# Gate half of a gated MLP's input projection with tokens on partitions: 16 of 48 weight pairs by seven products, results mixed and multiplied there, transposed afterwards

## The chip, the cores and the metric

One core of one Trainium2 chip runs the whole kernel. The metric is device time in microseconds (us) of one execution; lower is better. The time before is the median of three executions, 2474.93 us. Where the text speaks of "no change" it means within 0.2% of that, about 5 us.

## The reference, cut to what matters

Two layers of a trunk over 256 tokens of width 2048. Layer 0 mixes tokens with a spatial gating unit, layer 1 with latent attention; after each comes a gated MLP with a short convolution. The change is in layer 0's mixer alone:

```python
def gmlp_mixer(x, w_in, ln_g, ln_b, w_s, b_s, w_out):
    z = jax.nn.gelu(x @ w_in)                 # 256 x 2048 by 2048 x 12288
    u, v = jnp.split(z, 2, axis=-1)           # 256 x 6144 each
    v = layer_norm(v, ln_g, ln_b)
    v = v.reshape(B, S // GM_BLOCK, GM_BLOCK, GM_GROUPS, GM_GROUP_DIM)   # 2 windows of 128, 8 groups of 768
    w = w_s * mask[None]
    s = jnp.einsum('gij,bnjgd->bnigd', w, v) + jnp.transpose(b_s)[None, None, :, :, None]
    return (u * s.reshape(B, S, GM_HALF)) @ w_out
```

`u` is the gate half and `v` the value half. All products carry about float32 precision: each operand is split into a high and a low part of the type that the matrix engine takes in one pass (`F32R`), and three of the four part products are added: high by high, low by high, high by low.

## The kernel before

Weights stream from memory in chunks of 1 MB (128 partitions x 2048 numbers). `Feed` loads a chunk into `raw` (three buffers, SP's queue), ScalarE casts it to the high part (`wh`, line 128), and VectorE subtracts for the low part (`wl`, line 131). A chunk is split two chunks ahead of its use, into 14 buffers of 1 MB named `big`.

**The value half** (lines 705 to 743) runs in six groups `v0` to `v5` of 1024 columns, each with eight chunks (pairs of row blocks of 128). Tokens are the stationary operand and 512 weight columns move, so results have tokens on partitions: two token blocks by two column halves, four banks `q3`, `p2`, `e`, `q4`, which the code calls DIRECT. A plain pair (`Banks.eight`) is 8 block products of three matmuls, 24 matmuls. For 20 pairs of groups 1 to 5 a Strassen-like scheme with seven block products (`Banks.seven`, 21 matmuls) is used. It needs sums of weight blocks (line 138: `ts`, then `th`, `tl`), sums of token blocks made once (`xc`), four more banks (`p1`, `q5`, `p7`, `p6`, called OWN), and after a group's last such pair four VectorE operations that fold these banks (`rest`, lines 436 to 444). Group results go through Gelu into `v[g]`.

**The gate half** (lines 809 to 832) runs in twelve groups of 512 columns with four chunks each, the other way round (`prod_a`, line 369): weights are stationary and tokens move, so results have features on partitions. A block of 128 x 128 weights takes two matmuls: the high weights against 512 columns (high and low tokens), the low weights against 256. So a chunk is 32 matmuls, half of 512 and half of 256 columns. `sum_halves` adds the two halves. Every second group, `spatial` mixes 1024 columns of `v` by 16 products of 128 columns (tile `s`); `scaled` applies the layer norm's gain and bias per feature (a column of `cst`) and the spatial bias, and line 830 multiplies by the gate, into `pT`, which has features on partitions, as the output projection (`down`, tag `wo`) wants its stationary operand.

Between the halves stand one transpose of the layer norms' rows (line 746), and two products of 512 columns for row sums of the spatial weights (line 753).

The order on each engine is made by the framework's scheduler from the program order and dependencies; an engine then executes its list in order. PSUM has eight banks, given out in rotation by `bank`; a matmul into a bank waits until the readers of its former contents are done. Small tiles rotate too: `t1` (6 buffers), `t2` (5 buffers of 128 x 512).

Of the kernel before, what the change touches and what calls it, by code (L numbers as in the profile page):

```python
# [8 lines left out]
F32 = mybir.dt.float32  # L9
# [40 lines left out]
V_SEVEN = [()] + [(2, 3, 4, 6)] * 5  # L50

# [22 lines left out]
class Feed:  # L74
# [59 lines left out]
    def _seven(self, i, raw):  # L134
# [13 lines left out]
        self.sums = last if i >= 48 else None  # L148
# [64 lines left out]
def trunk(ctx: ExitStack, tc: tile.TileContext, x, xT, gm_in, gm_wout, ffn_up, ffn_dn,  # L213
# [37 lines left out]
    chunks += [(gm_in[i], 2048, "") for i in range(48, gm_in.shape[0])]  # L251
# [34 lines left out]
    def turn(t, k1, k2):  # L286

        b0, b1 = slice(0, P), slice(P, S)
        tc.keep_in_program_order(nc.vector.tensor_tensor(t[:, 0], k1[:, b0], k1[:, b1], ALU.subtract))
        nc.vector.tensor_tensor(t[:, 1], k1[:, b1], k2[:, b1], ALU.subtract)  # L290
        nc.vector.tensor_tensor(t[:, 2], t[:, 1], k1[:, b0], ALU.subtract)
        nc.vector.tensor_tensor(t[:, 3], k2[:, b0], t[:, 2], ALU.add)
# [113 lines left out]
    class Banks:  # L406


        def __init__(self, tag, names):
            self.tag, self.begun = tag, set()  # L410
            self.acc = {n: bank(f"{tag}_{n}") for n in names}
# [5 lines left out]
        def eight(self, a, hi, lo):  # L417

            for b in range(2):
                for f in range(2):  # L420
                    for j in range(len(a[b])):
                        self.to(DIRECT[2 * b + f], a[b][j], hi, lo, j * 1024 + f * 512)

        def seven(self, a, sums, wh, wl, th, tl, turned=0):
            s1, s2, s3, s4 = sums
            self.to("q3", s4, wh, wl, 512)
            self.to("p2", a[0][1], wh, wl, 1024)
            self.to("p1", a[0][0], wh, wl, 0)
# [17 lines left out]
    class Acts:  # L446
# [5 lines left out]
        def make(self, u, kind, tag="big"):  # L452
# [4 lines left out]
            x = self.src[u // 4][:, 2 * u % 8 : 2 * u % 8 + n, :]  # L457
# [17 lines left out]
            nc.scalar.copy(hi, x)  # L475
            tc.keep_in_program_order(nc.vector.tensor_tensor(lo, x, hi.bitcast(F32), ALU.subtract))
# [4 lines left out]
    def down(n_k, src, tag, ln, acts, skew=SKEW):  # L481
# [6 lines left out]
        for hf, units in enumerate(seq):  # L488
            n = len(units)
            last = [u for u, kind in units if kind != "wide"][-1]  # L490
            acc = Banks(f"{tag}{hf}", OWN + DIRECT if hf else DIRECT + OWN)
            for i, (u, kind) in enumerate(units):
# [6 lines left out]
                if left == 6:  # L499
                    ln.prep()  # L500
                a, sums = acts.got[u]
# [202 lines left out]

    for gi in range(6):

        acc = Banks(f"v{gi}", DIRECT if gi == 0 else DIRECT + OWN if gi % 2 else OWN + DIRECT)
        rest = (None,) * 4
        for c, p in enumerate(V_PAIRS[gi]):
# [14 lines left out]
            if c == 4 and gi == 5:  # L724
                wT = slot([P, 2, 1024], "wT")
                wTg = wT[:, 0, :].rearrange("p (g i) -> p g i", g=NG)
                nc.sync.dma_start(wTg, w_sT)
                nc.sync.dma_start(wT[:, 1, :], b_s.to_broadcast([P, 1024]))
                nc.gpsimd.memset(wTg[64:P, :, 0:64], 0.0)
# [8 lines left out]
        if gi == 0:  # L738
            nc.sync.dma_start(cst, consts)
            nc.sync.dma_start(rope_sb, ropes)  # L740

            lnrow = tp.tile([P, P], F32, tag="t1", name="lnrow", bufs=T1)
            nc.sync.dma_start(lnrow, ln_rows.rearrange("r (k p) -> (r k) p", p=P))
    stats(5)
    lnt = bank("lnrowT")
    nc.tensor.transpose(lnt[:, 0:P], lnrow, ident)
    nc.scalar.copy(lncol, lnt[:, 0:P])
    rsum = slot([P, 1024], "rsum")
    ones = tp.tile([P, P], F32, tag="t1", name="ones", bufs=T1)
    nc.gpsimd.memset(ones, 1.0)  # L750
# [16 lines left out]
    def norm_v(gi, b):  # L767
# [4 lines left out]
    for b in range(2):  # L772
        norm_v(0, b)
# [35 lines left out]
    for gi in range(12):  # L809
        acc = [bank(f"u{gi}_{f}") for f in range(4)]  # L810
        for c in range(4):
            hi, lo = feed.next()
            prod_a(acc, xhl, range(4 * c, 4 * c + 4), hi, lo)
            if gi > 0:
                next(jobs, None)
# [465 lines left out]
```

## Time and profile before

| what | us |
|---|---|
| median of three executions | 2474.93 (2474.13 to 2475.21) |
| profiled execution, its own time | 2475.22 |
| span of the profile | 2473.0 |
| value half, groups 1 to 5 (first matmul of `v1` to the transpose of line 746) | 50.77 to 254.77 |
| gate half with what stands between (to the first matmul of `wo`) | 254.77 to 544.87, 290.10 |

PE is TensorE, PEld its weight loads, DVE VectorE, ACT ScalarE, POOL GpSimd, SP the engine that issues most transfers. A matmul's listed duration is its latency, and successive ones overlap; its cost in a stream is the distance between starts. The same holds, less strongly, for DVE and ACT. The timeline merges equal neighbours ("x32") and gives the start of the first and the time to the end of the last.

### The profile page before, as it was taken

Reading aid. Unit: us, or ns where it says so; the run is one execution under the profiler, and the core shown is the slowest. Engines: PE = TensorE matmul, PEld = TensorE weight load, DVE = VectorE, ACT = ScalarE, POOL = GpSimd, SP = SyncE. Lnnn points to the kernel's source line nnn. Section 1 sums busy time; section 2 is a strip of 40 time slices with the busy share of each in tenths; the row PEclk is TensorE's granted clock in tenths of the full one; section 3 lists DMA queues with packets and bytes.
Section 4 is the critical chain, followed back from the end, with each engine's and each line's share of the span. In section 5 each row is a group of like instructions: output and inputs, shape, how many; then the busy total and the mean of one; then the engine's idle time right before and its main releaser. Section 6 shows DMA issues by size and latency. Waiting matters only on the chain. (4 is left out here: it accounts for less than half of the span.)

```text
span 2473.0 us, 33399 instructions
## 1 busy us (share of the span) xinstructions
PE 2460.1 (99%) x12947; PEld 2118.2 (86%) x12947; DVE 1992.8 (81%) x2786; ACT 1425.3 (58%) x1995; POOL 88.3 (4%) x171
## 2 busy tenths in 40 slices
PE   9999999999999999999999999999999999999998
PEld 7888888888888888888888888988888888888886
DVE  7999866679898788788777897866688787878798
ACT  6666544456565656566654466565565665655453
POOL 0000000000000000000000000000000000000000
PEclk9999999999999999999999999999999999999999
DMA  7556544556665678777868885544478787877885
GB/s 281 204 204 218 207 171 171 178 187 215 204 204 204 215 297 323 296 279 288 330 217 325 302 296 191 191 156 158 173 271 314 268 312 293 301 265 277 297 324 199
DMA packets 108990, 606.15 MB, mean 245 GB/s; under 512 B 10272, under 2 KB 11040, under 8 KB 61600
## 3 DMA queue, kind: packets, MB, share of 16 engines
q1 hardware_dynamic: 84832, 463.51, 52.8%
q0 software_dynamic: 24000, 140.52, 14.9%
q8 instruction: 101, 1.65, 0.3%
q14 instruction: 57, 0.47, 0.1%
HBM read 538.98 MB, written 65.01 MB: 244 GB/s over the span
## 5 line engine op out<-in xcount | busy, mean ns | idle before, releaser
L131 DVE TENSOR_TENSOR wl<-raw,wh 128x1024 fp32r<-128x1024 f32 (+4 forms) x693 | 971.9, 1420 | 237.6 <-ACT wh L128 140.2
L128 ACT CAST wh<-raw 128x1024 fp32r<-128x1024 f32 (+4 forms) x693 | 820.7, 1211 | 405.6 <-PE u L233 99.7
L233 PE MATMUL up<-xhl,wh 128*128 128x512 f32 x2624 | 611.3, 390 | 0.0
L233 PEld LDWEIGHTS up<-xhl,wh 128*128 128x128 f32 x2624 | 487.4, 188 | 97.7
L233 PEld LDWEIGHTS up<-xhl,wl 128*128 128x128 f32 x2624 | 325.8, 192 | 6.4
L233 PE MATMUL up<-xhl,wl 128*128 128x256 f32 x2624 | 328.1, 283 | 0.0
L233 PE MATMUL u<-xhl,wh 128*128 128x512 f32 x768 | 180.8, 391 | 0.0
L233 PEld LDWEIGHTS u<-xhl,wh 128*128 128x128 f32 x768 | 142.2, 188 | 28.6 <-DVE v L734 0.2
L128 ACT CAST th<-ts 128x1536 fp32r<-128x1536 f32 x106 | 110.1, 1052 | 87.8 <-DVE ts L138 63.7
L131 DVE TENSOR_TENSOR tl<-ts,th 128x1536 fp32r<-128x1536 f32 x106 | 125.4, 1219 | 8.0 <-PE dn_p L233 3.4
L233 PEld LDWEIGHTS u<-xhl,wl 128*128 128x128 f32 x768 | 95.3, 192 | 1.9
L233 PE MATMUL u<-xhl,wl 128*128 128x256 f32 x768 | 95.9, 283 | 0.0
L233 PE MATMUL mo<-wh,oT 128*128 128x512 f32 x256 | 82.4, 401 | 0.0
L138 DVE TENSOR_TENSOR ts<-ts,raw 128x512 f32<-128x512 f32 x106 | 72.8, 687 | 0.9
L233 PE MATMUL v_q<-wh,xhl 128*128 128x512 f32 x224 | 69.9, 393 | 0.4 <-ACT wh L128 0.4
L138 DVE TENSOR_TENSOR ts<-raw 128x1024 f32<-128x1024 f32 x53 | 64.6, 1219 | 1.2 <-PE wo_q L233 1.0
L233 PE MATMUL v_p<-wh,xhl 128*128 128x512 f32 x192 | 59.7, 390 | 0.6 <-ACT wh L128 0.6
L233 PEld LDWEIGHTS mo<-wh,oT 128*128 128x128 f32 x256 | 45.5, 189 | 7.1
L233 PEld LDWEIGHTS v_q<-wh,xhl 128*128 128x128 f32 x224 | 42.3, 189 | 9.7 <-ACT wh L128 1.1
L233 PE MATMUL mo<-wl,oT 128*128 128x512 f32 x128 | 50.0, 391 | 0.0
L682 ACT ACTIVATE lny<-lnt,lncol 128x128 f32<-128x128 f32 x96 | 36.5, 470 | 15.6 <-PE lnt L678 15.5
L155 DVE TENSOR_TENSOR praw<-praw 128x512 f32<-128x512 f32 x64 | 43.9, 686 | 0.6
(1703 smaller groups left out, 4142.8 us busy)
## 6 DMA issues: line engine op xcount, KB each, us to landing
raw<-in_ffn_up_dram SPq DMA_DIRECT2D x172, 1024.0 KB, 7.0
raw<-in_gm_in_dram SPq DMA_DIRECT2D x93, 1024.0 KB, 4.9
raw<-in_ffn_dn_dram SPq DMA_DIRECT2D x68, 1024.0 KB, 6.8
raw<-in_gm_wout_dram SPq DMA_DIRECT2D x48, 1024.0 KB, 5.4
praw<-in_ffn_dn_dram POOLq DMA_DIRECT2D x16, 1024.0 KB, 14.8
keptth<-pth POOLq DMA_DIRECT2D x16, 1024.0 KB, 8.2
kepttl<-ptl POOLq DMA_DIRECT2D x16, 1024.0 KB, 9.2
fth<-keptth POOLq DMA_DIRECT2D x16, 1024.0 KB, 9.6
```

The lines of the kernel that those rows point to most:

```text
L128: cast = self.nc.scalar.copy(hi, raw)
L131: self.nc.vector.tensor_tensor(lo, raw, hi.bitcast(F32), ALU.subtract)
L138: add = lambda o, a, b: self.nc.vector.tensor_tensor(o, a, b, ALU.add)
L155: add = lambda o, a, b: pin(nc.vector.tensor_tensor(o, a, b, ALU.add))
L233: recent[0] = nc.tensor.matmul(o, l, r, start=start, stop=stop, skip_group_check=True)
L682: nc.scalar.activation(y[:, j], t[:, j * P : (j + 1) * P], AF.Identity, bias=lncol[:, o : o + 1], scale=lncol[:, g : g + 1])
```

## The change

The gate half gets the value half's form. Its 48 weight chunks become six groups of eight pairs, with tokens stationary and 512 weight columns moving; 16 pairs use seven products. A chunk's data is the same, but a pair is now gathered from two stored chunks, in pieces of 1024 numbers instead of rows of 2048. Results have tokens on partitions. So the layer norm's gain and bias become rows: `cst`'s columns are transposed once after `v0`, written to memory (`gbd`), and read back as rows spread over 128 partitions, two of 256 KB for each half group (`row_v`, POOL's queue, tiles of `t2`). `norm_v` applies mean, deviation, gain and bias to `v[g]` in place (eight VectorE operations a group in place of one for each token block). `spatial` makes the spatial weights stationary and moves 512 (or twice 256) columns of `v`; ScalarE adds the spatial bias on the way out of PSUM. The product with the gate goes into `v[g]`, and one group later `turned` transposes its 16 blocks of 128 x 128, and ScalarE copies them back to `v[g]`, which takes `pT`'s place. The eight banks `ub` are used by turns: a group's DIRECT banks are the next group's OWN banks, and `spatial` and `turned` use the OWN banks before the first seven-product pair does. The row sums and `scaled` are gone. The transposes of line 746's kind move to the end of `v0`, in four banks given out there.

```diff
+U_PAIRS = [[0, 1, 5, 7, 2, 6, 3, 4]] + [[0, 1, 2, 5, 3, 7, 4, 6]] * 5
+U_SEVEN = [(2, 3)] + [(2, 3, 4)] * 4 + [(2, 3)]
...
-    chunks += [(gm_in[i], 2048, "") for i in range(48, gm_in.shape[0])]
+    for g in range(6):
+        for p in U_PAIRS[g]:
+            i = 48 + 8 * g + p // 2
+            w = gm_in[i : i + 5 : 4, :, p % 2 * 1024 : p % 2 * 1024 + 1024].rearrange("f p c -> p f c")
+            chunks.append((w, 2048, "seven" if p in U_SEVEN[g] else "wide"))
...
     for gi in range(6):
 
-        acc = Banks(f"v{gi}", DIRECT if gi == 0 else DIRECT + OWN if gi % 2 else OWN + DIRECT)
+        acc = Banks(f"v{gi}", DIRECT if gi == 0 else OWN + DIRECT if gi % 2 else DIRECT + OWN)
...
+            if c == 4 and gi == 0:
+                nc.sync.dma_start(cst, consts)
+                nc.sync.dma_start(rope_sb, ropes)
+                nc.sync.dma_start(lnrow, ln_rows.rearrange("r (k p) -> (r k) p", p=P))
+                nc.sync.dma_start(brow[0:NG, :], b_s.rearrange("o (g i) -> (o g) i", g=NG))
...
         if gi == 0:
...
+            lnt, bst, gbt = bank("lnrowT"), bank("brT"), bank("gbT")
+            bank("spare")
+            nc.tensor.transpose(gbt[0:96, 0:P], cst[:, C_GMG : C_GMG + 96], ident)
+            nc.tensor.transpose(lnt[:, 0:P], lnrow, ident)
+            nc.tensor.transpose(bst[:, 0:NG], brow[0:NG, :], ident[0:NG, 0:NG])
+            gbs = tp.tile([P, P], F32, tag="t1", name="gbs", bufs=T1)
+            nc.scalar.copy(gbs[0:96, :], gbt[0:96, 0:P])
+            nc.gpsimd.dma_start(gbd.rearrange("r (f c) -> (r f) c", c=P), gbs[0:96, :])
+            nc.scalar.copy(lncol, lnt[:, 0:P])
+            nc.scalar.copy(bsc, bst[:, 0:NG])
     stats(5)
-    lnt = bank("lnrowT")
-    nc.tensor.transpose(lnt[:, 0:P], lnrow, ident)
-    nc.scalar.copy(lncol, lnt[:, 0:P])
...
-    for f in range(2):
-        rb = bank(f"rows{f}")
-        mm(rb, ones, wT[:, 0, f * 512 : (f + 1) * 512], True, True)
-        nc.scalar.copy(rsum[:, f * 512 : (f + 1) * 512], rb)
...
+    def row_v(g, f):
+
+        got = []
+        for i in range(2):
+            t = tp.tile([P, 512], F32, tag="t2", name=f"vr{g}{f}{i}", bufs=T2)
+            nc.gpsimd.dma_start(t, gbd[12 * i + 2 * g + f : 12 * i + 2 * g + f + 1, :].to_broadcast([P, 512]))
+            got.append(t)
+        return got
+
+    def norm_v(g, f, rows):
+
+        for b in range(2):
+            t = v[g][:, b, f * 512 : (f + 1) * 512]
+            nc.vector.scalar_tensor_tensor(t, t, mv[b][:, 0:1], rows[0], ALU.subtract, ALU.mult)
+            nc.vector.scalar_tensor_tensor(t, t, vrs[b], rows[1], ALU.mult, ALU.add)
...
+    ub = [bank(f"ub{i}") for i in range(8)]
+
+    def spatial(g, tiles):
+
+        for i, t in enumerate(tiles):
+            b, f = i // 2, i % 2
+            n = 2 * g + f
+            cuts = [(0, 512)] if n % 3 != 1 else [(0, 256), (256, 512)]
+            for o, e in cuts:
+                h = (512 * n + o) // 768
+                mm(t[:, o:e], wTg[h], v[g][:, b, f * 512 + o : f * 512 + e], True, True)
+            for o, e in cuts:
+                h = (512 * n + o) // 768
+                nc.scalar.activation(v[g][:, b, f * 512 + o : f * 512 + e], t[:, o:e], AF.Identity,
+                                     bias=bsc[:, h : h + 1])
+
+    def turned(g, tiles):
+
+        for i, t in enumerate(tiles):
+            src = v[g][:, i // 2, i % 2 * 512 : i % 2 * 512 + 512]
+            for j in range(4):
+                nc.tensor.transpose(t[:, j * P : (j + 1) * P], src[:, j * P : (j + 1) * P], ident)
+            nc.scalar.copy(src, t)
...
+    for g in range(6):
+        direct, own = (ub[4:], ub[:4]) if g % 2 else (ub[:4], ub[4:])
+        acc = Banks(f"u{g}", DIRECT + OWN, direct + own)
+        for c, p in enumerate(U_PAIRS[g]):
+            a = [[x_parts(xhl, 2 * p + j, b) for j in range(2)] for b in range(2)]
+            got = feed.next()
+            if p in U_SEVEN[g]:
+                acc.seven(a, xc[p], *got, turned=512, across=True)
+                if p == U_SEVEN[g][-1]:
+                    rest = acc.rest()
+            else:
+                acc.eight(a, *got, across=True)
+            if c == (0 if g else 2):
+                spatial(g, own)
+            if c == 1 and g:
+                turned(g - 1, own)
+            if c == 1 and g < 5:
+                rows = row_v(g + 1, 0)
+            if c in (3, 5) and g < 5:
+                norm_v(g + 1, c // 4, rows)
+                if c == 3:
+                    rows = row_v(g + 1, 1)
+            if c in (4, 5, 6) and g == 5:
+                acts.make(*plan(NF_GM)[0][c - 4])
+        for n, t in zip(DIRECT, rest):
+            nc.vector.tensor_tensor(t, acc.acc[n], t, ALU.add)
+            nc.scalar.activation(t, t, AF.Gelu_apprx_tanh)
+        for i, t in enumerate(rest):
+            o = v[g][:, i // 2, i % 2 * 512 : i % 2 * 512 + 512]
+            nc.vector.tensor_tensor(o, o, t, ALU.mult)
 
     ln = Norm(0, {})
-    acc, end = down(NF_GM, pT, "wo", ln, acts)
+    acc, end = down(NF_GM, pT, "wo", ln, acts, tiles=ub, beside=lambda: turned(5, ub[4:]))
```

The order of instructions moves at three places that matter. In the rows below a name's last number is the program's own count; `[waits X]` names the engines or queues on whose semaphores the row waits.

On PE, at the end of `v0`: before, the first matmuls of `v1` follow at once.

```order
L233 MATMUL v0_q4_203<-wl7_348,xhl0_3_87 128x512
L233 MATMUL v1_q3_463<-wh8_377,xhl0_0_84 128x512 [waits Activation_49]
L233 MATMUL v1_q3_463<-wh8_377,xhl0_0_84 128x512
L233 MATMUL v1_q3_463<-wl8_378,xhl0_0_84 128x512 [waits DVE_49]
L233 MATMUL v1_q3_463<-wh8_377,xhl0_0_84 128x512 x2
L233 MATMUL v1_q3_463<-wl8_378,xhl0_0_84 128x512
L233 MATMUL v1_p2_464<-wh8_377,xhl0_0_84 128x512 x2
```

After the change three transposes stand between, and `v1`'s first three banks are theirs: `q3` and `p2` wait for ScalarE at their first matmul.

```order
L236 MATMUL v0_q4_207<-wl7_356,xhl0_3_87 128x512
L762 MATMUL gbT_469<-ident_186,cst_183 96x128 [waits DMAHW0_49,Pool_49]
L763 MATMUL lnrowT_467<-ident_186,lnrow_200 128x128 [waits DMAHW2_49]
L764 MATMUL brT_468<-ident_186,brow_201 128x8 [waits DMAHW3_49]
L236 MATMUL v1_q3_483<-wh8_385,xhl0_0_84 128x512 [waits Activation_49]
L236 MATMUL v1_q3_483<-wh8_385,xhl0_0_84 128x512
L236 MATMUL v1_q3_483<-wl8_386,xhl0_0_84 128x512 [waits DVE_49]
L236 MATMUL v1_q3_483<-wh8_385,xhl0_0_84 128x512 x2
L236 MATMUL v1_q3_483<-wl8_386,xhl0_0_84 128x512
L236 MATMUL v1_p2_484<-wh8_385,xhl0_0_84 128x512 [waits Activation_49]
```

On ACT, at the same place, after the change: the copies that empty those banks stand behind the last Gelu of `v0` and a cast; before, the cast `wh10` followed the cast `th9` directly.

```order
L756 ACTIVATE v0_462,vsum_197<-v0_e_206 128x512 [waits PE_49]
L756 ACTIVATE v0_462,vsum_197<-v0_q4_207 128x512 [waits PE_49]
L131 CAST th9_425<-ts9_422 128x512 [waits DVE_49]
L766 COPY gbs_474<-gbT_469 96x128 [waits PE_49]
L768 COPY lncol_185<-lnrowT_467 128x128 [waits PE_49]
L769 COPY bsc_202<-brT_468 128x8 [waits PE_49]
L131 CAST wh10_487<-raw10_389 128x2048 [waits DMAHW5_49]
```

So the release of `q3`'s bank moved behind a Gelu that itself follows `v0`'s last matmul.

On DVE, in the second gate group (`u1`; chunk 56 is its first pair, chunk 58 its first with seven products), after the change: the last product of group 0 with its gate (line 863), then the split of chunk 58, then the norm of `v2` with its rows `vr200` and `vr201`, and chunk 59's low parts among it.

```order
L863 TENSOR_TENSOR v0_462<-v0_462,u0u3_2305 128x512 [waits Activation_49]
L134 TENSOR_TENSOR wl58_2357<-raw58_2280,wh58_2356 128x1536
L141 TENSOR_TENSOR ts58_2355<-ts58_2355,raw58_2280 128x512 [waits DVE_49]
L134 TENSOR_TENSOR tl58_2359<-ts58_2355,th58_2358 128x1536 [waits PE_49,Activation_49]
L134 TENSOR_TENSOR tl58_2359<-ts58_2355,th58_2358 128x512 [waits Activation_49]
L796 SCALAR_TENSOR_TENSOR v2_1077<-v2_1077,vmv0_2005,vr200_2453 128x512 [waits DMASW5_49]
L796 SCALAR_TENSOR_TENSOR v2_1077<-v2_1077,vmv1_2006,vr200_2453 128x512
L797 SCALAR_TENSOR_TENSOR v2_1077<-v2_1077,vrs0_2015,vr201_2455 128x512 [waits DMASW6_49,DVE_49]
L134 TENSOR_TENSOR wl59_2404<-raw59_2317,wh59_2403 128x2048 [waits DMAHW6_49,Activation_49]
```

Before, the gate half's list on DVE held low parts, norms of 1024 columns and operations of 128 or 256 columns, and nothing in it waited for POOL's queue; now the first row of line 796 does (`DMASW`), with the low parts of chunk 59 behind it.

More of the change, by code (lines that the diff above doesn't have):

```diff
@@ L806, in park_all @@
             yield
-    jobs = park_all(feed.used + 48 + 2 * len(PLAN[NF_GM][0].split()))
[L809 to L815, printed above, removed]
-            if gi % 2 == 0 and gi < 10 and c in (1, 2):
-                norm_v(gi // 2 + 1, c - 1)
-        if gi == 11:
-            for t in plan(NF_GM)[0][:2]:
-                acts.make(*t)
-        if gi % 2 == 0:
-            sp = spatial(gi // 2)
-        hs = [sum_halves(acc[f], f"u{4 * gi + f}") for f in range(4)]
-        for h in hs:
-            nc.scalar.activation(h, h, AF.Gelu_apprx_tanh)
-        if gi % 2 == 0:
-            scaled(gi // 2, sp)
-        for f, h in enumerate(hs):
-            t = pT[gi // 2][:, 4 * (gi % 2) + f, :]
-            nc.vector.tensor_tensor(t, t, h, ALU.mult)
-        if gi == 10:
-            acts.make(*plan(NF_GM)[0][2])
+    for g in range(6):
[28 more added lines that the diff above has]
+            nc.vector.tensor_tensor(o, o, t, ALU.mult)
```

94 lines of the change are left out of this document (36 added, 58 removed).

## The prediction

> **What bounds the kernel now.** I read the page's head and chain of waits first, then the busy time by windows, one in the value half and one in the gate half, then timelines and groups for prices.
>
> ```profile
> span 2473.0 us, 33399 instructions
> PE 2460.1 (99%) x12947; PEld 2118.2 (86%) x12947; DVE 1992.8 (81%) x2786; ACT 1425.3 (58%) x1995; POOL 88.3 (4%) x171
> ...
> PE 34%; DVE 0%; DVEq 0%; issue 0%
> ```
>
> ```profile
> 60.00:250.00 190.00, 190.00 (x839) 157.31 (x839) 182.55 (x164) 125.60 (x147) 0.53 (x1) 1.00 0.60 212
> 290.00:540.00 250.00, 250.00 (x1495) 223.28 (x1494) 162.12 (x259) 108.69 (x166) 0.84 (x1) 1.00 0.53 183
> ```
>
> The columns of the windows are PE, PEld, DVE, ACT and POOL busy, the granted clock, and the transfers' share. PE has no idle time in either half, at full clock, and it alone is on the chain. So the time is the sum of PE's stream, plus any wait that the change puts into it. VectorE differs: 182.55 of 190 us (96%) in the value half, whose form the change copies, 162.12 of 250 (65%) in the gate half. The value half shows that this form can run with PE never waiting.
>
> **The change part by part.** First the price of a 512-column matmul in the value half's form:
>
> ```profile
> 50.77 0.62 PE L233 MATMUL v_q<-wh,xhl 128*128 128x512 f32 x2
> ...
> 254.77 0.27 PE L746 MATMUL lnrowT<-ident,lnrow 128*128 128x128 f32 x1
> ```
>
> Groups 1 to 5 begin at 50.77 and end at 254.77. Each has four pairs of 24 and four of 21 matmuls, 180; 204.0 us over 900 is 0.2267 us each. Next the gate half as it is:
>
> ```profile
> 260.26 4.00 PE L233 MATMUL u<-xhl,wl 128*128 128x256 f32 x32
> 264.09 7.44 PE L233 MATMUL u<-xhl,wh 128*128 128x512 f32 x32
> 271.37 4.00 PE L233 MATMUL u<-xhl,wl 128*128 128x256 f32 x32
> ...
> 278.86 3.73 PE L233 MATMUL s<-wT,v 128*128 128x128 f32 x32
> ...
> 544.87 0.62 PE L233 MATMUL wo_q<-wh,wo0wx 128*128 128x512 f32 x2
> ```
>
> Here 32 matmuls of 512 columns take 7.28 us (264.09 to 271.37), 0.2275 each, but 32 of 256 columns take 3.83 us, 0.1197 each, more than half of 0.2267: the narrow ones are dear. A chunk (16 of each) costs 5.56 us; a plain pair in the new form moves the same columns in 24 x 0.2267 = 5.44, a seven-product pair in 21 x 0.2267 = 4.76. **Removed:** all from 254.77 to 544.87, 290.10 us. **Added for products:** 32 x 24 + 16 x 21 = 1104 matmuls, 250.3 us.
>
> The mixing by the spatial weights and the transposes:
>
> ```profile
> L233 PE MATMUL rows<-wT,ones x4: 592/592/593, 254.9 to 256.2; 128*128 128x512 f32 x4
> ```
>
> ```profile
> 1595.30 1.04 PE L1029 MATMUL qrt<-ident,qrs 128*128 128x128 f32 x8
> ...
> L1029 PE MATMUL qrt<-ident,qrs x32: 272/272/273, 1595.3 to 1616.2; 128*128 128x128 f32 x32
> ```
>
> A full float32 product of 512 columns is issued as two matmuls (two calls of line 753, four rows), whose starts are 1.3 us / 3 = 0.43 apart. The mixing now needs 24 banks of 512 columns: 24 x 0.86 = 20.6 us (before, 32 narrow ones a group, (3.73 - 0.28) / 31 = 0.111 each, 21.4 in all, inside the 290.10). I take cut banks (twice 256 columns) at the same price. A transpose of 128 x 128 costs (1.04 - 0.27) / 7 = 0.11, and the gate half adds 96: 10.5 us. New gate half: 250.3 + 20.6 + 10.5 = 281.4, a gain of 8.7 us. The three transposes at the end of `v0` add 0.3.
>
> **The wait at the end of `v0`.** By the order rows, `v1`'s first matmul waits until ScalarE has copied `lncol`, behind the last Gelu of `v0`, the cast `th9` and the copy `gbs`:
>
> ```profile
> 51.88 0.61 ACT L735 ACTIVATE v<-v_q 128x512 f32<-128x512 f32 x1
> 52.36 0.22 ACT L735 ACTIVATION_READ_ACCUMULATOR v<-v_q 128x1 f32 x1
> 52.45 0.64 ACT L128 CAST th<-ts 128x512 fp32r<-128x512 f32 x1
> 52.96 1.94 ACT L128 CAST wh<-raw 128x2048 fp32r<-128x2048 f32 x1
> ...
> 255.08 0.27 ACT L747 COPY lncol<-lnrowT 128x128 f32<-128x128 f32 x1 [5.79 <-PE lnrowT L746]
> ```
>
> PE would be ready at 50.77 + 0.3 = 51.1. ScalarE's last Gelu started at 51.88, and the operation after `th9` at 52.96; there two copies of 0.27 now stand, so the bank is free at about 53.5. PE waits 2.4 us. Bounds: nothing, if the wait named is only for a cast long done, and 3.3 if the copies take their full length one after another behind the whole cast (52.45 + 0.64 + 2 x 0.27 = 53.6) and signals add as much again as one of them. I take 2.4, since ScalarE's list is in order and its timeline gives the place. What is queued behind the copies is the cast `wh10`, needed only by the third pair of `v1`. `cst` is no new wait: its load was issued at 34.68 and took 6.4 us:
>
> ```profile
> 34.68 0.43 SPq L739 DMA_DIRECT2D cst<-in_consts_dram  x1
> ...
> cst<-in_consts_dram SPq DMA_DIRECT2D x1, 396.0 KB, 6.4
> ```
>
> **What I cost at nothing, and its cover.** VectorE, by the value half's groups:
>
> ```profile
> L131 DVE TENSOR_TENSOR wl<-raw,wh 128x2048 fp32r<-128x2048 f32 x18 | 40.9, 2289 | 1.1 <-ACT wh L128 0.3
> L131 DVE TENSOR_TENSOR tl<-ts,th 128x1536 fp32r<-128x1536 f32 x19 | 33.3, 1755 | 2.2 <-PE v_p L233 1.5 <-ACT th L128 0.4
> L131 DVE TENSOR_TENSOR wl<-raw,wh 128x1536 fp32r<-128x1536 f32 x19 | 33.3, 1753 | 2.1 <-PE v_q L233 2.0 <-PE v_p L233 0.2
> L138 DVE TENSOR_TENSOR ts<-ts,raw 128x512 f32<-128x512 f32 x36 | 24.8, 689 | 0.7
> L138 DVE TENSOR_TENSOR ts<-raw 128x1024 f32<-128x1024 f32 x18 | 21.9, 1219 | 0.2 <-PE v_q L233 0.2
> L131 DVE TENSOR_TENSOR tl<-ts,th 128x512 fp32r<-128x512 f32 x19 | 13.0, 684 | 0.0
> ...
> 254.26 0.68 DVE L734 TENSOR_TENSOR v<-v_q,v5w 128x512 f32<-128x512 f32 x1
> 254.87 0.68 DVE L734 TENSOR_TENSOR v<-v_p,v5p 128x512 f32<-128x512 f32 x1
> ...
> L667 DVE SCALAR_TENSOR_TENSOR res<-res,lnmv,lng 128x512 f32<-128x512 f32 x8 | 5.7, 744 | 0.1
> ```
>
> Two additions of 0.68 start 0.61 apart, so an operation costs its length less 0.07. A seven-product chunk is 1.22 + 2 x 0.69 + 2 x 1.75 + 0.68 - 6 x 0.07 = 6.4 us, a plain one 2.2. A gate group with three of the first and five of the second, twelve folding operations (four in `rest`, four additions, four products with the gate) of 0.61, and eight of the norm at 0.67 comes to 19.2 + 11.0 + 7.3 + 5.4 = 42.9 us. PE's group is 183 x 0.2267 + 3.4 + 1.8 = 46.7. VectorE is at 92%, below the 96% at which the value half ran without a wait, with 3.8 us to spare a group. Were the cover gone, each us beyond 3.8 would cost PE one. ScalarE has more room (three times 3.6, five times 1.9, some 8 us of copies and Gelus: 28 of 46.7).
>
> Within a group the waits have room too. `spatial` stands one plain pair (5.4 us) after the group's start, and its banks are free after four additions (2.4). `turned` stands 14.3 us after it (two pairs and `spatial`), its products with the gate are done after some 5. Its four copies run behind PE's last blocks, and the first seven-product matmul into an OWN bank comes 1.4 us later. So I add nothing.
>
> Loads: a chunk in pieces, and the rows.
>
> ```profile
> raw<-in_gm_in_dram SPq DMA_DIRECT2D x93, 1024.0 KB, 4.9
> raw<-in_gm_wout_dram SPq DMA_DIRECT2D x48, 1024.0 KB, 5.4
> ...
> praw<-in_ffn_dn_dram POOLq DMA_DIRECT2D x16, 1024.0 KB, 14.8
> ...
> lnp<-in_ln_rows_dram POOLq DMA_DIRECT2D x8, 256.0 KB, 5.0
> ```
>
> `wout` comes in the same pieces and lands 0.5 us later, with three buffers ahead: nothing. A row of the norm is like `lnp`, 5.0 us, against 14.8 for the worst transfer of POOL's queue.
>
> **Sum**, against the profiled execution's 2475.22 us: -8.7 + 0.3 + 2.4 = -6.0, so 2469.2; the median of the three runs is 0.3 lower, 2468.9. I predict 2469.
>
> **The rivals.** *No wait at the end of `v0`:* 2466.5. For it: the value half never waited. Against: the order rows.
>
> *Small waits at the group starts.* If VectorE reaches the four additions late, `spatial` waits. At 1 us for each of five starts: 2474. For it: 92% busy on average says nothing of the worst place. Against: 3 us of room there.
>
> *The rows arrive late (the slower side).* The first row tile of the next group is free only after a product with the gate, some 4 us into a group; at 5.0 us it lands at 9, when VectorE, after the split of chunk 58 (4.6 us), asks for it. The norm waits in order, and behind it are the low parts of the next pairs, which PE waits for. Up to 3.8 us late costs nothing; landing after 9 us instead of 5 decides. At 12 us it is 3 us in each of four groups: 2481; at 14.8, 2492. For it: POOL's queue does show 14.8. Against: that was a transfer four times as large.
>
> *Transposes at full length.* If each cost its listed 0.272 us, 96 would be 26.1, 15.6 more: 2485. Against it: eight in a row start 0.11 apart, with the clock at 1.00:
>
> ```profile
> 1594.00:1597.00 3.00, 3.00 (x28) 3.00 (x27) 2.57 (x6) 1.86 (x6) 0.00 (x0) 1.00 0.96 325
> ```
>
> [...]
>
> **How the numbers follow.** Forecast 0.55, no wait at `v0` 0.06, small waits 0.23, late rows 0.13, long transposes 0.03. A measurement of this kernel tells 0.2% (5 us, 2470.0) from no change. Faster: the first two, less the forecast's edge over 2470 (0.03), 0.58. Slower (over 2479.9): late rows and long transposes and a little, 0.17. Same: 0.25. The range runs from the bound without the wait to beyond the small waits: 2466 to 2477.
>
> **What would show it.** In the new profile: 1104 matmuls into `ub` at 0.2267; PE idle once, some 2.4 us near 51, released by ScalarE's `lncol`; the gate half some 281 us long; transposes 0.11 apart; VectorE near 92% there; no PE wait on `v` or `ub`. PE idle at line 236 with a release by `ub` copies, or DVE waiting for `vr`, or a gate half over 285 us, would make the prediction wrong.

## The result and the profile after

The changed kernel takes 2469.52 us (median of 11 runs, 2468.82 to 2472.34), the kernel before 2474.88 us (11 runs, 2474.13 to 2475.92). The ratio is 0.998, with a 95% interval of 0.9972 to 0.9988: 5.4 us less, by the medians just over the 0.2% that counts as a difference here, though the interval reaches below it. The forecast was 2469. That the two agree to 0.5 us is partly luck: one term of the sum did not happen, and another wait of nearly its size did.

From the page of the changed kernel: the span, the busy time of each engine with its instructions, and the head of the chain that ended last.

```profile
span 2469.5 us, 32459 instructions
...
PE 2453.7 (99%) x12481; PEld 2091.0 (85%) x12481; DVE 2054.2 (83%) x2734; ACT 1459.5 (59%) x1969; POOL 104.2 (4%) x202
...
PE 34%; DVE 0%; DVEq 0%; issue 0%
```

PE still sets the time. VectorE went from 81% to 83%, and PE's instructions from 12947 to 12481. The same windows as before (PE, PEld, DVE, ACT and POOL busy, granted clock, transfers); the second window ends 10 us earlier, since the half does:

```profile
60.00:250.00 190.00, 190.00 (x839) 157.38 (x839) 182.73 (x165) 125.76 (x147) 0.40 (x2) 1.00 0.58 205
290.00:530.00 240.00, 237.99 (x1065) 193.17 (x1064) 219.90 (x218) 143.14 (x148) 8.58 (x16) 1.00 0.62 203
```

VectorE is at 219.90 of 240 us, the 92% of the forecast. PE is idle for 2.0 us in the gate half, which it never was before. The list of PE's waits (waiting line, releaser, us in total, times, longest) names that place and two at the start, of which the last, 1.3 us, is there before the change too:

```profile
PE ub L236 <- DVE u0w L449: 1.9, 1, 1.9
PE v_q L236 <- ACT wh L131: 1.7, 1, 1.7
PE warm L236 <- POOL idle L286: 1.3, 1, 1.3
```

No wait for `lncol` is among them. To see where the time went, the execution is cut at five starts of PE: the end of `v0` (first of the three transposes; before, `v1`'s first matmul), the first matmul into `ub` (before, the transpose of line 746), the first with `wo0wx` (the next projection), the first with `wo2sx` (ahead of which, after the change, the last 16 transposes run), and PE's last matmul. All numbers are us of one profiled execution each, except the medians:

| kernel | median | profiled | to the end of `v0` | `v1` to `v5` | gate half to `wo0wx` | `wo0wx` to `wo2sx` | rest of PE |
|---|---|---|---|---|---|---|---|
| before | 2474.88 | 2475.22 | 50.77 | 204.00 | 290.10 | 10.88 | 1906.39 |
| changed | 2469.52 | 2471.25 | 52.89 | 204.60 | 282.54 | 12.55 | 1906.06 |
| `e1_again` | 2469.42 | 2468.97 | 51.23 | 204.60 | 281.69 | 12.55 | 1906.27 |
| `e2_early_rows` | 2466.66 | 2468.64 | 52.78 | 204.60 | 279.94 | 12.55 | 1906.16 |
| `e3_no_seven` | 2479.26 | 2478.11 | 51.09 | 204.60 | 290.82 | 12.55 | 1906.15 |
| `e4_double_turn` | 2479.75 | 2479.64 | 51.18 | 204.60 | 290.77 | 14.30 | 1906.18 |
| `e5_four_seven` | 2465.88 | 2465.88 | 51.05 | 204.60 | 277.96 | 12.55 | 1907.10 |
| `e6_pad5` | 2468.26 | 2468.20 | 52.41 | 204.60 | 279.94 | 12.55 | 1906.08 |
| `e7_pad10` | 2469.59 | 2469.59 | 52.49 | 204.60 | 281.19 | 12.55 | 1906.12 |
| `e8_no_lead` | 2467.69 | 2468.26 | 52.49 | 204.60 | 279.94 | 12.55 | 1906.06 |
| `e9_pad15` | 2481.02 | 2480.93 | 51.02 | 204.60 | 293.91 | 12.55 | 1906.25 |
| `e10_late_rows` | 2500.89 | 2501.68 | 52.42 | 204.60 | 312.45 | 12.55 | 1907.07 |
| `e11_best` | 2466.06 | 2466.31 | 52.47 | 204.60 | 277.22 | 12.55 | 1906.86 |

The table is the main tool of what follows. Where PE waits for nothing a stage repeats to hundredths (204.60 in all twelve profiles after the change, 279.94 in three different kernels), and there a few tenths can be read from one profile each. Where PE waits it does not: the gate half of the changed kernel is 282.54 us in one profile and 281.69 in the other, so differences below 0.9 us between kernels with waits show nothing for certain. The medians cannot be read so finely: the first 53 us alone differ by 1.9 us between profiles.

For the change as a whole (both profiled executions): +2.1 to the end of `v0`, +0.6 in `v1` to `v5` with the three transposes, -7.6 to `wo0wx`, +1.7 beside `wo0` for the last 16 transposes, -0.3 in the rest, and 0.5 less outside PE's span. That is -4.0, and -5.4 in the medians; this profile has a slow start, and with the start of `e1_again` it would be near -5.6.

### The profile page after: what moved, and what is told of

The parts are those of the page before. It is cut to its first block, busy times and chain, and to the rows that moved or that the text cites. A ratio compares the mean times of both kernels' runs of the same rounds, so it can differ in the third digit from the quotient of the medians.

```text
span 2469.5 us, 32459 instructions
## 1 busy us (share of the span) xinstructions
PE 2453.7 (99%) x12481; PEld 2091.0 (85%) x12481; DVE 2054.2 (83%) x2734; ACT 1459.5 (59%) x1969; POOL 104.2 (4%) x202
## 5 line engine op out<-in xcount | busy, mean ns | idle before, releaser
L134 DVE TENSOR_TENSOR wl<-raw,wh 128x1024 fp32r<-128x1024 f32 (+4 forms) x645 | 957.3, 1499 | 176.8 <-ACT wh L131 131.8
L131 ACT CAST th<-ts 128x1536 fp32r<-128x1536 f32 (+1 forms) x138 | 142.8, 1052 | 113.8 <-DVE ts L141 89.4
L236 PE MATMUL ub<-wh,xhl 128*128 128x512 f32 x576 | 179.5, 393 | 1.9 <-DVE u0w L449 1.9
L134 DVE TENSOR_TENSOR tl<-ts,th 128x1536 fp32r<-128x1536 f32 (+1 forms) x138 | 162.9, 1217 | 10.5 <-ACT th L131 3.6
L236 PEld LDWEIGHTS ub<-wh,xhl 128*128 128x128 f32 x576 | 108.1, 188 | 26.4 <-DVE u0w L449 2.4
L236 PE MATMUL ub<-wl,xhl 128*128 128x512 f32 x288 | 112.2, 389 | 0.0
L141 DVE TENSOR_TENSOR ts<-ts,raw 128x512 f32<-128x512 f32 x138 | 94.5, 684 | 1.4
L141 DVE TENSOR_TENSOR ts<-raw 128x1024 f32<-128x1024 f32 x69 | 84.0, 1218 | 7.7 <-PE ub L236 3.8
L236 PEld LDWEIGHTS ub<-wl,xhl 128*128 128x128 f32 x288 | 54.1, 188 | 11.4
L396 DVE TENSOR_TENSOR h_0a<-up,lo_0a 128x256 f32<-128x256 f32 x41 | 17.2, 419 | 32.7 <-ACT lo_0a L394 32.7
```

What stands on the lines that cost most here:

```text
L131: cast = self.nc.scalar.copy(hi, raw)
L134: self.nc.vector.tensor_tensor(lo, raw, hi.bitcast(F32), ALU.subtract)
L141: add = lambda o, a, b: self.nc.vector.tensor_tensor(o, a, b, ALU.add)
L236: recent[0] = nc.tensor.matmul(o, l, r, start=start, stop=stop, skip_group_check=True)
L396: nc.vector.tensor_tensor(h, acc[:, 0:S], lo, ALU.add)
```

## The experiments

Eleven more runs were made, the first of the changed kernel itself. Where medians differ by less than the scatter of the start, the stages of the table are read instead.

**The changed kernel again**, with nothing edited.

> The changed kernel once more, nothing edited, for a second profile. Question: is the 2.1 us by which the first profile's v0 ended later (52.89 against 50.77 us) a property of the change or scatter of the first loads? Theory scatter: the change does not touch the order of SP's loads before 23 us, so this profile shows another time of the first group's end, within some 2 us of either, and the median is 2469.5 again. Rival, the change delays the start: the first group ends near 52.9 again and the spread of the times stays narrow. Both theories expect the second gate group's start to wait 1.9 us again.

Measured: 2469.42 us (2468.43 to 2471.81); `v0` ends at 51.23, and the second gate group waits 1.5 us. So the 2.1 us at the start are scatter. The timelines of PE show how it comes about: first of the changed kernel's profile, then of this one (start, duration, operation; in brackets the idle time and its releaser).

```profile
6.89 0.40 PE L236 MATMUL v_e<-wh,xhl 128*128 128x512 f32 x1
9.00 1.22 PE L236 MATMUL v_q<-wh,xhl 128*128 128x512 f32 x2 [1.72 <-ACT wh L131]
10.02 0.63 PE L236 MATMUL v_p<-wl,xhl 128*128 128x512 f32 x1
10.45 0.63 PE L236 MATMUL v_p<-wh,xhl 128*128 128x512 f32 x1
```

```profile
7.90 0.40 PE L236 MATMUL v_e<-wh,xhl 128*128 128x512 f32 x1
8.92 0.74 PE L236 MATMUL v_q<-wh,xhl 128*128 128x512 f32 x2 [0.62 <-ACT wh L131]
9.50 0.40 PE L236 MATMUL v_p<-wl,xhl 128*128 128x512 f32 x1
9.73 0.40 PE L236 MATMUL v_p<-wh,xhl 128*128 128x512 f32 x1
```

The same matmul starts at 9.00 and 8.92, but in the first profile it comes after 1.72 us of waiting and those behind it start 0.43 us apart instead of 0.23, until about 12.5 us. Seven matmuls at that pace, 0.2 us more each, lose 1.4 us of the 1.7 by which the two profiles differ at the end of `v0`. The granted clock shows it too: 0.51 from 9.0 to 12.5 us in the first profile, 1.00 in the second. The moved loads of `cst`, `rope_sb`, `lnrow` and `brow` are not issued before 29.73 us in the profile of the change, so they cannot be the cause.

**The first rows early.** The two row pairs for `v0`'s norm get a buffer of their own and are loaded at the start of `v5`:

```diff
+            if c == 0 and gi == 5:
+                rows0 = slot([P, 4, 512], "rows0")
+                for n in range(4):
+                    r = 12 * (n % 2) + n // 2
+                    nc.gpsimd.dma_start(rows0[:, n], gbd[r : r + 1, :].to_broadcast([P, 512]))
...
-    for f, rows in enumerate([row_v(0, 0), row_v(0, 1)]):
-        norm_v(0, f, rows)
+    for f in range(2):
+        norm_v(0, f, [rows0[:, 2 * f], rows0[:, 2 * f + 1]])
```

> The rows of gamma and beta for the first gate group are loaded into a buffer of their own at the start of v5, some 40 us before they are used. Theory: VectorE stood 3.0 us (266.5 to 269.7 us) for these rows, worked without a gap from there to 302 us, so freed the raw buffers late; the load of the next chunk came late, VectorE stood for it (302.9 to 305.1) ahead of the folding u0w, and PE waited 1.9 us at the second group's start. With the rows there the wait goes: 2.0 us less than the changed kernel, near 2467.5, and no PE wait on u0w. Rival: the first group simply has too much VectorE work (the norm of two groups, 16 operations, and small ones), so the wait stays at 1.5 us or more and the time within 0.5 us of 2469.5.

Measured: 2466.66 us, ratio to before 0.9968 (0.9957 to 0.998); gate half 279.94 against 281.69 and 282.54, and no wait on `u0w`. The theory holds. (The edit also takes four tiles out of the rotation of `t2`, so the rows of the second group come earlier too; the two were not tried apart.) What happens without the edit stands in the changed kernel's timelines. VectorE, at the first norm and at the end of group 0:

```profile
269.73 0.75 DVE L796 SCALAR_TENSOR_TENSOR v<-v,vmv,vr 128x512 f32<-128x512 f32 x1 [3.03 <-DMA vr<-gbrows]
...
295.64 6.70 DVE L134 TENSOR_TENSOR wl<-raw,wh 128x2048 fp32r<-128x2048 f32 x3
302.26 0.68 DVE L448 TENSOR_TENSOR u0u<-ub,u0p 128x512 f32<-128x512 f32 x1
305.08 1.22 DVE L141 TENSOR_TENSOR ts<-raw 128x1024 f32<-128x1024 f32 x1 [2.15 <-DMA raw<-in_gm_in_dram]
306.23 0.68 DVE L449 TENSOR_TENSOR u0w<-ub,u0u 128x512 f32<-128x512 f32 x1
```

PE at the same place:

```profile
304.64 0.39 PE L236 MATMUL ub<-wl,xhl 128*128 128x512 f32 x1
306.97 0.73 PE L236 MATMUL ub<-wh,xhl 128*128 128x512 f32 x2 [1.94 <-DVE u0w L449]
```

And VectorE with the early rows:

```profile
291.91 2.29 DVE L134 TENSOR_TENSOR wl<-raw,wh 128x2048 fp32r<-128x2048 f32 x1
294.80 4.50 DVE L134 TENSOR_TENSOR wl<-raw,wh 128x2048 fp32r<-128x2048 f32 x2 [0.59 <-ACT wh L131]
299.21 0.68 DVE L448 TENSOR_TENSOR u0u<-ub,u0p 128x512 f32<-128x512 f32 x1
299.82 1.23 DVE L141 TENSOR_TENSOR ts<-raw 128x1024 f32<-128x1024 f32 x1
300.96 0.68 DVE L449 TENSOR_TENSOR u0w<-ub,u0u 128x512 f32<-128x512 f32 x1
```

Read it as a chain. The rows come 3.0 us late. VectorE then works on without catching up, and the first of the three low parts `wl` starts at 295.64 instead of 291.91. That operation reads chunk 55 and frees its raw buffer, into which chunk 58 is loaded, so this load is issued some 3.7 us later (298.0 instead of 294.3). In VectorE's list the split of chunk 58 (`ts`) stands between two foldings, `u0u` and `u0w`. It waits 2.15 us for its load, and `u0w`, which needs no load at all, waits behind it. PE needs the bank that `u0w` reads. Three us at one place became two at another, 37 us later.

Why the rows were late is in the row of POOL's queue (changed kernel):

```profile
259.57 1.06 POOL L788 DMA_DIRECT2D vr<-gbrows  x2 [198.74 <-ACT vsq L713]
```

The loads had stood at the head of POOL's queue for 199 us, but their tiles (tag `t2`) are those into which `stats(5)` writes its squares, which ScalarE does only among and after the last Gelus of `v5`.

**No seven-product pairs in the gate half.** `U_SEVEN` is empty, and the Gelu reads the four banks directly.

```diff
-U_SEVEN = [(2, 3)] + [(2, 3, 4)] * 4 + [(2, 3)]
+U_SEVEN = [()] * 6
...
-        for n, t in zip(DIRECT, rest):
-            nc.vector.tensor_tensor(t, acc.acc[n], t, ALU.add)
-            nc.scalar.activation(t, t, AF.Gelu_apprx_tanh)
+        rest = [tp.tile([P, 512], F32, tag="t2", name=f"u{g}{n}", bufs=T2) for n in DIRECT]
+        for n, t in zip(DIRECT, rest):
+            nc.scalar.activation(t, acc.acc[n], AF.Gelu_apprx_tanh)
```

> All 48 pairs of the gate half with eight products; no seven-product pair, and no folding. PE issues 48 matmuls more at 0.2267 us: +10.9 us. VectorE has much less to do there, so the wait of 2.0 us at the second group's start goes. Theory (the gate half is PE's stream, 0.2267 a matmul): 2469.5 + 10.9 - 2.0 = 2478.4. Rival (VectorE's load costs PE more than the listed wait, through many small gaps): less than 2476.

Measured: 2479.26 us; gate half 290.82. Against the kernel whose second group does not wait (279.94) that is 10.88 us for 48 matmuls, 0.2267 each, to the last digit the price that the prediction took. It also says what the layout is worth by itself: gate half and the block behind it take 303.4 us, against 301.0 before. Without the seven-product pairs the change loses 2.4 us there.

**Transposes twice.**

```diff
-            for j in range(4):
+            for j in (0, 1, 2, 3, 0, 1, 2, 3):
```

> Each of the 96 transposes of the products is issued twice (same result written again). Theory: a transpose costs PE 0.109 us, so +10.5 us, 2480.0. Rival, the price is the listed length of 0.272 us: +26 us, 2495.6. A third possibility, hidden: the copies from the banks wait longer and the next blocks with them, +12 to +15.

Measured: 2479.75 us. Gate half and next block are 10.83 us longer than in `e1_again`, 0.113 us for each of 96 transposes, though each is listed with 273 ns:

```profile
L825 PE MATMUL ub<-ident,v x192: 270/273/273, 317.8 to 560.8; 128*128 128x128 f32 x192
```

The rival of long transposes is out. ScalarE's copies, which wait for the blocks (3.9 us in nine places, 1.7 in one without the edit), cost PE nothing.

**A fourth seven-product pair** in groups 1 to 4, on top of the early rows:

```diff
-U_PAIRS = [[0, 1, 5, 7, 2, 6, 3, 4]] + [[0, 1, 2, 5, 3, 7, 4, 6]] * 5
-U_SEVEN = [(2, 3)] + [(2, 3, 4)] * 4 + [(2, 3)]
+U_PAIRS = [[0, 1, 5, 7, 2, 6, 3, 4]] + [[0, 1, 2, 3, 5, 4, 6, 7]] * 4 + [[0, 1, 2, 5, 3, 7, 4, 6]]
+U_SEVEN = [(2, 3)] + [(2, 3, 4, 6)] * 4 + [(2, 3)]
```

> With the early rows, gate groups 1 to 4 have four seven-product pairs (2, 3, 4, 6) as the value half has, in the order 0 1 2 3 5 4 6 7. PE issues 12 matmuls less: -2.7 us. VectorE has 4.2 us more in each of these groups: 47.1 us against PE's 46.0. Theory (VectorE has 3.8 us to spare a group and costs PE what lies beyond): 1.1 us of waiting in each of four groups, so 2466.7 - 2.7 + 4.4 = 2468.4. Rival (room is larger than the sum of lengths says, as in the value half at 96%): no wait, 2464.0.

Measured: 2465.88 us, gate half 277.96, 1.98 less than with the early rows alone, of the 2.72 us that 12 matmuls are worth. VectorE did not cost the 4.4 us of the theory:

```profile
290.00:530.00 240.00, 239.97 (x1074) 194.56 (x1073) 234.32 (x242) 149.68 (x156) 8.57 (x16) 1.00 0.61 202
```

It is at 98% in this window, and PE still hardly waits: none is listed, and most of the missing 0.7 us lies in a few matmuls with `tl` or behind one, which start 0.31 to 0.42 us after the one before instead of 0.23. So the 3.8 us to spare a group, as the prediction used them, are too few. The rest of PE is 0.9 us longer in this profile. Nearly all of that is one wait at 2433 us, in the last projection of the program (0.5 us for VectorE's `dn13wx`, the matmul 0.7 us late); the profile of `e10_late_rows` has the same wait, so it does not come from this edit.

**More work for VectorE.** Additions on a scratch tile, one, two or three after each of pairs 1 to 5 in groups 1 to 4, on top of the early rows (the lines for five a group; ten and fifteen have `range(2)` and `range(3)`):

```diff
+    pad = st.tile([P, 512], F32, tag="pad", name="pad", bufs=1)
+    nc.vector.memset(pad, 0.0)
...
+            if 1 <= g <= 4 and 1 <= c <= 5:
+                for _ in range(1):
+                    tc.keep_in_program_order(nc.vector.tensor_tensor(pad, pad, pad, ALU.add))
```

> With the early rows, five additions of 128x512 on a scratch tile are given to VectorE in each of gate groups 1 to 4, one after each of pairs 1 to 5: 5 x 0.61 = 3.05 us a group. Theory (3.8 us to spare a group): no change, 2466.7. Rival (what counts is the fullest place in a group, not the sum): 2 us or more above it.

> The same with ten additions, 6.1 us a group. Theory (3.8 us to spare a group, beyond it each us costs PE one): 2.3 us in each of four groups, 2466.7 + 9.2 = 2475.9. Rival (idle time of 3.1 us that the trace shows in these groups is not all usable): 3 us or more a group, 2479 and above.

> With the early rows, fifteen additions of 128x512 on a scratch tile in each of gate groups 1 to 4, 9.0 us a group. Theory now (VectorE's own idle time of 21.6 us in the 240 us from 290 to 530 is 4.2 a group, and besides it may fall about one pair, some 6 us, behind once before PE meets it): 36 - 17 - 6 = 13 us, gate half 293 us instead of 279.9, time near 2479.7. Rival (the prediction's price, 3.8 us of room and then one for one): 4 x 5.2 = 21 us, gate half 301, 2487.5.

Measured, gate half: 279.94 with five (not a hundredth more; the median's 2468.26 is the start's scatter), 281.19 with ten (+1.25), 293.91 with fifteen (+13.97). So 12 us of extra work cost nothing, 24 us cost 1.25, and the next 12 us cost 12.7. Once VectorE has no more room, one us of its work lengthens the gate half by about one, as the prediction had it. The room is larger than it said: about 23 us over four groups, 5.7 a group instead of 3.8. One part of it can be read. The window of the early rows shows VectorE idle for 21.6 of 240 us, 4.2 a group:

```profile
290.00:530.00 240.00, 240.00 (x1077) 195.52 (x1076) 218.43 (x221) 142.10 (x148) 8.57 (x16) 1.00 0.61 203
```

That is 17 us of the 23. The other 6 would fit VectorE falling behind by about a pair, once, before PE meets it; this is inferred from the difference, not measured. The same window with ten additions, then with fifteen:

```profile
290.00:530.00 240.00, 239.17 (x1071) 194.14 (x1071) 237.58 (x256) 139.50 (x145) 8.57 (x16) 1.00 0.61 200
```

```profile
290.00:530.00 240.00, 232.18 (x1015) 186.18 (x1014) 236.42 (x261) 133.43 (x139) 8.58 (x16) 0.98 0.56 183
```

At 237.58 of 240 us, 99%, PE lost 0.83 us. With fifteen additions VectorE's busy share does not rise; PE's falls, and so does the granted clock, to 0.98. How the 14 us come about is not told by the sum alone: the listed waits of PE are only 7.8 us, and after the two longest it runs at half pace, which takes some 1.7 and 2.4 us more (on the clock, see below). VectorE is idle for only 5 us of the whole 293.91, so the total follows its work; whether the slow matmuls add to that, or only stand in for waits that would have come later, this run does not separate. So the 13 us of the last expectation came out close without its account being shown in full.

**Rows asked for later.** On top of the early rows, the row loads of groups 1 to 5 are written where the norm uses them:

```diff
-            if c == 1 and g < 5:
-                rows = row_v(g + 1, 0)
             if c in (3, 5) and g < 5:
-                norm_v(g + 1, c // 4, rows)
-                if c == 3:
-                    rows = row_v(g + 1, 1)
+                norm_v(g + 1, c // 4, row_v(g + 1, c // 4))
```

> With the early rows, the rows of groups 1 to 5 are loaded where the norm uses them, two pairs later than in the changed kernel. Theory (the rival of late rows was a real danger): each norm waits some 5 us for its rows, twice a group, VectorE has 3.8 to spare, so 6.2 us in each of five groups: 2466.7 + 31 = 2497.7. Rival (the work that is written ahead of the norm in VectorE's list covers the load): less than 2472.

Measured: gate half 279.94, no change. But this run decides nothing, since the loads do not go later. POOL's queue with the early rows, and with this edit on top:

```profile
302.54 0.54 POOL L793 DMA_DIRECT2D vr<-gbrows  x1 [38.16 <-DVE u0u L450]
```

```profile
302.87 0.54 POOL L793 DMA_DIRECT2D vr<-gbrows  x1 [38.77 <-DVE u0u L450]
```

POOL has nothing else to do (busy for 8.57 of 240 us with the early rows), so a load starts when its tile comes free, wherever it is written: the next seven loads, up to 353 us, also start within 0.4 us of each other in the two profiles. Both theories took the place in the program for the time of the transfer.

**Late rows, forced.** On top of the early rows for the first group, into each later row's tile row 0 of the table is loaded twice ahead of the right row, each load behind the one before:

```diff
             t = tp.tile([P, 512], F32, tag="t2", name=f"vr{g}{f}{i}", bufs=T2)
+            for _ in range(2):
+                nc.gpsimd.dma_start(t, gbd[0:1, :].to_broadcast([P, 512]))
```

> With the early rows for the first group, each row of groups 1 to 5 is loaded three times into the same place, one after another, so that the second row lands some 10 us after VectorE asks for it (near 324 instead of before 314 us in the second group). It is the prediction's late-row rival made to happen. Its own price (room of 3.8 us, then one for one): 6.5 us in each of four groups, 26 us, 2492.7. Theory now (4.2 us of room and a lag of some 6 us once): 4 x 10.3 - 17 - 6 = 18 us, 2484.9. Third: VectorE's later list hides it, under 5 us.

Measured: 2500.89 us, gate half 312.45, 32.5 us longer; all three theories are too low. VectorE's and PE's waits:

```profile
DVE v L803 <- DMA vr<-gbrows: 21.8, 5, 6.9
DVE v L804 <- DMA vr<-gbrows: 19.8, 4, 6.3
```

```profile
PE ub L236 <- DVE wl L134: 18.4, 5, 5.0
PE ub L236 <- DVE u0w L449: 2.3, 1, 2.3
...
PE ub L236 <- DVE tl L134: 1.1, 1, 1.1
...
PE ub L236 <- DVE u2w L449: 0.6, 1, 0.6
PE ub L236 <- DVE u4w L449: 0.3, 1, 0.3
```

VectorE stands 41.6 us for rows, and PE 22.7 us behind it. This is not far from the 41.6 - 17 = 25 us that are left after VectorE's own idle time; the lag of 6 us would make it less, and is not to be seen here; that a stall in one piece, in the middle of a group's splits, leaves no room for it is a guess. Most of the other 9.8 us is not waiting. After the longer waits PE runs slowly:

```profile
435.63 0.61 PE L236 MATMUL ub<-wh,xhl 128*128 128x512 f32 x2
441.23 0.54 PE L236 MATMUL ub<-wl,xhl 128*128 128x512 f32 x1 [4.99 <-DVE wl L134]
441.57 1.05 PE L236 MATMUL ub<-wh,xhl 128*128 128x512 f32 x2
442.43 0.63 PE L236 MATMUL ub<-wl,xhl 128*128 128x512 f32 x1
442.85 1.06 PE L236 MATMUL ub<-wh,xhl 128*128 128x512 f32 x2
...
444.98 0.39 PE L236 MATMUL ub<-wl,xhl 128*128 128x512 f32 x1
```

The eight matmuls from 441.57 on start 0.427 us apart, where they take 0.227: 1.6 us on top of the wait, and there are four such waits.

**The best of these together**: early rows, four seven-product pairs in groups 1 to 4, three in the last group (the edit is against `e5_four_seven`).

```diff
-U_SEVEN = [(2, 3)] + [(2, 3, 4, 6)] * 4 + [(2, 3)]
+U_SEVEN = [(2, 3)] + [(2, 3, 4, 6)] * 4 + [(2, 3, 4)]
```

> Early rows, four seven-product pairs in gate groups 1 to 4 and a third one in the last group, which has no norm to do. Against the kernel with early rows 15 matmuls less, -3.4 us; group by group VectorE is at 98% in groups 1 to 4. Theory (VectorE's lag is given back in the last group): gate half 277.9 - 0.7 = 277.3 us, time 2465.2. Rival (the lag meets the splits of the next projection, which stand in VectorE's list in the last group): gate half 278 or more, 2466 or above.

Measured: gate half 277.22, as the theory had it (277.3). The median of six executions is 2466.06; one of them took 5298.52 us, which nothing here explains, and the median of the other five is 2465.81, ratio to before 0.9962 (0.9949 to 0.9975), with `v0` ending at 52.47 in the profile. `e5_four_seven` has 2465.88 and 0.9965 (0.9951 to 0.9979). Which of the two is faster their times cannot say. The gate half is 0.74 us shorter, near the 0.68 of three matmuls, but both kernels have short waits there, so one profile each does not prove it. Both kernels are below the changed one's median by about 3.5 us and below before by about 9.

## Why the prediction was near, step by step

- **The gate half's sum was right.** With the second group's wait gone (`e2_early_rows`), gate half and the transposes in the next block take 279.94 + 12.55 - 10.88 = 281.61 us; the prediction said 281.4. `e3_no_seven` measured the product at 0.2267 us (predicted 0.2267), `e4_double_turn` the transpose at 0.113 (predicted 0.11). The mixing follows from the total: 281.61 - 250.3 - 10.8 = 20.5 for 20.6.
- **The wait at the end of `v0` (+2.4) did not happen; this step failed.** The prediction took `v1`'s first wait on ScalarE for one on the copy of `lncol`. The timelines of the change, PE and then ScalarE:

```profile
52.89 0.27 PE L762 MATMUL gbT<-ident,cst 128*96 128x128 f32 x1
52.99 0.27 PE L763 MATMUL lnrowT<-ident,lnrow 128*128 128x128 f32 x1
53.20 0.22 PE L764 MATMUL brT<-ident,brow 8*128 8x8 f32 x1
53.35 0.73 PE L236 MATMUL v_q<-wh,xhl 128*128 128x512 f32 x2
```

```profile
55.23 0.28 ACT L768 COPY lncol<-lnrowT 128x128 f32<-128x128 f32 x1
```

  `v1`'s matmul starts 1.9 us before that copy. The order rows name the engine that is waited for, not the instruction, and the document ahead of the prediction was wrong to say that the release of `q3`'s bank had moved behind the Gelu. In the built program the three transposes lie in banks 2, 3 and 4 and `v1_q3` in bank 0, which `v0` does not use; nor are the transposes' banks those of `v1`'s `p2` and `e` (7 and 1), as was said there. The lower bound given for this term (a wait for a cast long done) came true. Its upper bound, 3.3 us, does not come out of its own figures: with one copy's 0.27 for the signals, 53.6 + 0.27 - 51.1 is 2.8. The place costs 0.46 us for the transposes, 0.16 more than predicted, and the stage with them is 0.60 us longer than before.
- **"Within a group the waits have room too ... So I add nothing" failed at one of five group starts**. The listed wait is 1.9 us in one profile and 1.5 in the other, and the gate half is 2.60 and 1.75 us longer than without it. The margins there assumed VectorE to be on time. They left out that the first group's rows wait for `t2` tiles, and that a folding can stand behind a split in VectorE's list. The rival of late rows had the mechanism (the norm waits in order, low parts behind it), but looked for it in groups 1 to 5, where the rows land in time: 4.1 us median in the changed kernel, 5.0 estimated. The rival of small waits looked at the group starts, but at all five and at the additions; it was one start, and a folding. Of the signs that were to make the prediction wrong, one is there: VectorE waited 3.0 us for `vr`, with PE's wait at line 236 behind it.
- **VectorE's load was right, its room was not.** 92% as worked out; but 3.8 us a group came from the sum of lengths, and 5.7 were there. The slope beyond it came out right as a sum: 12 us of work beyond the room cost 12.7, though part of that is PE at half pace.
- **The late rows as a danger were priced by the same small room and without the clock.** Forced (three loads one after another, 5.7 us each in the median), they cost 32.5 us, against 26 by the prediction's price; the runs show that a wait of several us also cost clock (0.64 in the 4.7 us that begin with the end of the 4.99 us wait in `e10_late_rows`).
- **The start was taken as a constant.** 50.77 us became 51.0 to 52.9 in twelve profiles. Whether the kernel before has slow starts too is open: only one profile of it was taken; its times reach 2477.43.

Put together, against the forecast's -6.0: -2.4 for a wait that was not there, +1.75 to +2.6 for one that was not seen, +0.3 in the stage with the three transposes, +0.2 in the gate half's own sum. That is -6.2 to -5.3, and -5.4 was measured. Two terms that were wrong cancelled each other to within 0.7 us; the remainder is the sum that the traces confirmed.

## What to carry to other kernels

A wait in an instruction list names an engine; before a price is put on it, find the buffer behind it and who held it last. When an engine is at 92%, ask not only how much room it has on average but what a single stall of it delays: here a buffer that came free late made a load late, and a result that needed no load stood behind it in the list. And read an edit's effect by stages between fixed points of the trace, which repeat to hundredths where nothing waits, rather than by medians that carry the scatter of the start.

## What the runs showed that was not expected

In the gate halves of two runs waits of PE had a second price. In all runs, waits there after which the next matmul started up to 2.7 us behind the one before were followed by matmuls at the usual pace (the granted clock was 1.00 from 307 to 309 us, behind the changed kernel's wait of 1.94 us); after such gaps of 3.4 to 5.4 us (four in `e10_late_rows`, two in `e9_pad15`) some 7 to 12 matmuls started 0.427 us apart. The window after the 5.4 us gap shows it as granted clock:

```profile
441.30:446.00 4.70, 4.70 (x14) 3.73 (x15) 4.70 (x6) 2.31 (x3) 0.00 (x0) 0.64 0.61 223
446.00:456.00 10.00, 10.00 (x46) 8.23 (x45) 9.93 (x11) 4.06 (x3) 0.00 (x0) 1.00 0.50 157
```

In `e9_pad15` the granted clock was 0.50 from 452 to 456 us, behind a wait of 3.94 us. Each such wait cost 1.4 to 2.4 us more than its own length; the time at half pace was 3 to 5 us.

At the start of the program shorter gaps were followed by half pace too. Of the twelve profiles after the change, six show a granted clock of 0.50 for 3.4 us somewhere between 7 and 12.5 us, and in these `v0` ends at 52.41 to 52.89; five show none and end at 51.02 to 51.23. The twelfth (`e8_no_lead`) ends at 52.49 without it, after two gaps of 1.9 us. This is most of the scatter of the start. The length of the gap alone does not decide: one of 1.85 us (`e7_pad10`) was followed by half pace, one of 2.08 (`e4_double_turn`) was not. None of the start's gaps reaches 3.4 us, the shortest in the gate halves that was followed by half pace. What does decide is open.
